# Loads on ACT's queue, stores on SyncE's queue, in a 180-degree rotation of images

## The chip, the cores and the metric

One core of one Trainium2 chip. The time is that of the core, in us of the device, measured over repeated executions; a profile is taken of one execution beside them and its span is about 2 us shorter than the time, since it begins with the first and ends with the last instruction. All runs quoted here are of the fast state, with a granted clock of 1.00, but for one execution, which is named where it comes.

## The reference

```python
batch, c, h, w = 32, 3, 256, 256          # float32
np.rot90(x, k=2, axes=(-2, -1))           # rotate every image by 180 degrees
```

Each of the 96 images of 65,536 elements is reversed as a flat list. 25.17 MB come in, 25.17 MB go out.

## The kernel before

A strip of 32 images lies in a tile of 128 partitions: each image is cut into 4 pieces of 16,384 elements (64 KiB), one per partition. Three strips (A, Bt, Ct) fill three tiles. VectorE reverses every partition in place, by swapping mirrored pieces of 2,048 elements through a small tile T. The store then puts the four pieces of an image in reversed order. Each tile is loaded once and stored once; no tile is used twice.

```python
    def load(t, g, lo, hi):
        return nc.sync.dma_start(out=t[:, lo:hi], in_=x4[g][:, lo:hi])

    def store(t, g):
        return nc.sync.dma_start(out=o4[g][:, ::-1, :], in_=t[:, :])

    def inside(t):                          # 12 copies on VectorE
        for lo in range(0, E // 2, J):
            hi = E - lo - J
            copy(T[:, :], back(t, hi, hi + J))
            copy(t[:, hi:hi + J], back(t, lo, lo + J))
            copy(t[:, lo:lo + J], T[:, :])

    TAIL = 1536
    load(A, 0, 0, E)
    load(Bt, 1, 0, E)
    body = load(Ct, 2, 0, E - TAIL)
    load(Ct, 2, E - TAIL, E)
    inside(A)
    first = store(A, 0)
    tc.add_manual_dep(                      # the hold: the first store waits for `body`
        first.ins, body.ins.name, ...)      # (arguments cut)
    for g, t in ((1, Bt), (2, Ct)):
        inside(t)
        store(t, g)
```

The load of Ct comes in two parts, a body of 58 KiB rows and a tail of 6 KiB rows. The first store is held until the body has landed, so that it gets going while the tail is on its way.

## Time and profile before

| | before |
|---|---|
| time, median of 6 runs | 122.25 us (122.0 to 122.47) |
| span of the profile | 120.2 us |
| DMA packets, share of 16 engines | 97.3%, one queue |
| VectorE busy | 37% |
| issue of the first store | 59.48 us |
| landing of the last store | 119.4 us |

In this trace a packet is one row of a transfer: the 1008 packets are 7 transfers of 128 rows and 112 packets of under 512 bytes. The prediction shows how the rows add up to the span. One more view is of use, the waits of SyncE's queue (columns: line, what it waited for, us in total, times, longest):

```profile
SPq L58 <- DMA Ct<-in_x_dram: 57.3, 2, 56.7
SPq L106 <- DMA out_dram<-Bt: 19.3, 1, 19.3
SPq L106 <- DMA out_dram<-Ct: 19.3, 1, 19.3
```

The first line is the hold: SyncE stands still for 56.7 us before it issues the first store. The other two are the end: the stores land one strip time, 19.3 us, apart.

### The profile page before, as it was taken

To read this page: it belongs to the slowest core of one execution; us is meant where nothing else is said; L and a number is where in the kernel's file an instruction comes from. 1 tells how busy PE (TensorE), PEld (TensorE's weight loads), DVE (VectorE), ACT (ScalarE), POOL (GpSimd) and SP (SyncE) were. 2 spreads that over 40 slices of the span, in tenths; PEclk is the share of its full clock that TensorE was granted. 3 is DMA by queue.
4 is the path that set the end of the run, shared out by engine and by line. 5 is a ranking of instruction groups with operands and counts; after the bars stand their busy time and mean duration, and the time that the engine had idled before them with its cause. 6 is when DMAs were issued, how large, how long until landed. Compare 5 with 4: busy or idle time off the path is not lost.

```text
span 120.2 us, 93 instructions
## 1 busy us (share of the span) xinstructions
DVE 44.2 (37%) x36; POOL 0.2 (0%) x4
## 2 busy tenths in 40 slices
DVE  0000000499995099999059999400000000000000
POOL 0000000000000000000000000000000000000000
DMA  9888988898889779779499888988898889888990
GB/s 349 349 349 371 676 349 349 371 676 349 349 349 698 316 316 632 316 336 613 202 408 698 349 349 349 698 349 349 349 698 349 349 349 698 349 349 349 632 414 0
DMA packets 1008, 50.33 MB, mean 419 GB/s; under 512 B 112, under 2 KB 112, under 8 KB 240
## 3 DMA queue, kind: packets, MB, share of 16 engines
q1 hardware_dynamic: 1008, 50.33, 97.3%
HBM read 25.17 MB, written 25.17 MB: 419 GB/s over the span
## 4 chain that ended last, share of the span: by engine, by line
DMA 34%; DVE 25%; another core or an unknown queue 4%; issue 1%; SPq 0%; DVEq 0%
DMA Bt<-in_x_dram 34%; DVE T L52 8%; DVE Bt L52 8%; DVE Ct L52 8%; SPq L55 0%; DVEq L52 0%
## 5 line engine op out<-in xcount | busy, mean ns | idle before, releaser
L52 DVE COPY T<-A 128x2048 f32<-128x2048 f32 x4 | 4.9, 1227 | 22.6 <-DMA A<-in_x_dram 22.5
L52 DVE COPY T<-Ct 128x2048 f32<-128x2048 f32 x4 | 4.9, 1227 | 4.5 <-DMA Ct<-in_x_dram 4.4
L52 DVE COPY T<-Bt 128x2048 f32<-128x2048 f32 x4 | 4.9, 1227 | 4.4 <-DMA Bt<-in_x_dram 4.3
L52 DVE COPY Bt<-T 128x2048 f32<-128x2048 f32 x4 | 4.9, 1227 | 0.1
L52 DVE COPY A<-T 128x2048 f32<-128x2048 f32 x4 | 4.9, 1227 | 0.1
L52 DVE COPY Ct<-T 128x2048 f32<-128x2048 f32 x4 | 4.9, 1227 | 0.1
L52 DVE COPY A<-A 128x2048 f32<-128x2048 f32 x4 | 4.9, 1227 | 0.1
L52 DVE COPY Bt<-Bt 128x2048 f32<-128x2048 f32 x4 | 4.9, 1227 | 0.1
L52 DVE COPY Ct<-Ct 128x2048 f32<-128x2048 f32 x4 | 4.9, 1226 | 0.1
L95 POOL MEMSET const-uint8-127<- 128x1 uint8 x1 | 0.1, 102 | 0.0
L95 POOL MEMSET const-bfloat16-1.0<- 128x1 bf16 x1 | 0.1, 101 | 0.0
L95 POOL MEMSET const-float32-0.0<- 128x1 f32 x1 | 0.1, 98 | 0.2 <-issue 0.2
L95 POOL MEMSET const-float32-1.0<- 128x1 f32 x1 | 0.1, 98 | 0.0
## 6 DMA issues: line engine op xcount, KB each, us to landing
Ct<-in_x_dram SPq DMA_DIRECT2D x1, 7424.0 KB, 57.7
Ct<-in_x_dram SPq DMA_DIRECT2D x1, 768.0 KB, 59.2
A<-in_x_dram SPq DMA_DIRECT2D x1, 21.8
Bt<-in_x_dram SPq DMA_DIRECT2D x1, 40.7
out_dram<-A SPq DMA_DIRECT2D x1, 21.3
out_dram<-Bt SPq DMA_DIRECT2D x1, 39.9
out_dram<-Ct SPq DMA_DIRECT2D x1, 42.9
```

The costliest lines, as they stand in the source:

```text
L52: tc.keep_in_program_order(nc.vector.tensor_copy(out=dst, in_=src))
L95: nc = _bacc.Bacc("TRN2", target_bir_lowering=False, num_devices=1)
```

## The change

Its intent: give loads and stores a queue each, so that neither stands behind the other. Order, sizes and the hold stay.

```diff
     def load(t, g, lo, hi):
-        return nc.sync.dma_start(out=t[:, lo:hi], in_=x4[g][:, lo:hi])
+        return nc.scalar.dma_start(out=t[:, lo:hi], in_=x4[g][:, lo:hi])
 
     def store(t, g):
-        return nc.sync.dma_start(out=o4[g][:, ::-1, :], in_=t[:, :])
+        return tc.keep_in_program_order(
+            nc.sync.dma_start(out=o4[g][:, ::-1, :], in_=t[:, :]))
```

The wrapper around the store keeps its place among the other instructions.

## The prediction

> **What bounds the kernel now.** I read the page from the top (busy time, the slices, the DMA queue), then the chain that ended last, then the issues with their landings, and last the windows around the two places that the change can touch: the first 2.6 us and the stretch from 58 to 61 us, where loading turns into storing.
>
> The head of the page and its DMA part:
>
> ```profile
> span 120.2 us, 93 instructions
> DVE 44.2 (37%) x36; POOL 0.2 (0%) x4
> q1 hardware_dynamic: 1008, 50.33, 97.3%
> HBM read 25.17 MB, written 25.17 MB: 419 GB/s over the span
> ```
>
> One queue carries all 50.33 MB, and its packets fill 97.3% of the time of the 16 DMA engines. VectorE, the only engine that computes, works 37%. So the bytes bound the kernel, not the copies. The part that lists the DMA issues, whose last number is us from issue to landing:
>
> ```profile
> Ct<-in_x_dram SPq DMA_DIRECT2D x1, 7424.0 KB, 57.7
> Ct<-in_x_dram SPq DMA_DIRECT2D x1, 768.0 KB, 59.2
> A<-in_x_dram SPq DMA_DIRECT2D x1, 21.8
> Bt<-in_x_dram SPq DMA_DIRECT2D x1, 40.7
> out_dram<-A SPq DMA_DIRECT2D x1, 21.3
> out_dram<-Bt SPq DMA_DIRECT2D x1, 39.9
> out_dram<-Ct SPq DMA_DIRECT2D x1, 42.9
> ```
>
> With the issue times of the timeline (loads at 0.73, 1.18 and, for both parts of Ct, from 1.64 on to about 2.1; stores at 59.48, 60.20, 76.51) the landings are: A 22.5, Bt 41.8, body of Ct 59.4, tail of Ct 61.3, then stores 80.8, 100.1, 119.4. Each strip takes 19.3 us, loading or storing. In the trace's DMA records one 65,536-byte row takes 2.42 us on its engine after the first few, and a strip gives each of the 16 engines 128 / 16 = 8 rows: 8 x 2.42 = 19.3. Six strips are 6 x 19.3 = 116 us. The other 4 us of the span are the start (first packet at about 1.7), slower first rows (up to 3.3 instead of 2.42 us) and the end (last landing 119.4, span end 120.2).
>
> The chain of waits shows the copies as a quarter of the span, and this must be read with care:
>
> ```profile
> DMA 34%; DVE 25%; another core or an unknown queue 4%; issue 1%; SPq 0%; DVEq 0%
> ```
>
> It follows Bt's load, then the copies in Bt and Ct, and breaks off at the last store. The copies of Ct end at 76.5, and store Ct is issued at once, but the engines are busy with store A until 80.8 and store Bt until 100.1. Store Ct needs its turn only at about 100. So Ct has some 100 - 76.5 - 1.1 (issue to first byte, below) = 22 us of slack, and the DVE share of this chain is not on the path that sets the end.
>
> The start, in the timeline and in windows (columns: stretch, length, DVE busy, POOL busy, clock, DMA share, GB/s; a packet is booked whole in the window in which it starts, so a share can exceed 1 and an empty window is not an idle engine):
>
> ```profile
> 0.73 0.39 SPq L55 DMA_DIRECT2D A<-in_x_dram  x1
> 1.40:1.60 0.20, 0.00 (x0) 0.00 (x0) 1.00 0.00 0
> 1.60:1.80 0.20, 0.00 (x0) 0.00 (x0) 1.00 2.95 983
> 1.80:2.00 0.20, 0.00 (x0) 0.00 (x0) 1.00 6.83 2294
> ```
>
> Issue at 0.73, first packets after 1.6: the DMA records put it at 1.03 us from issue to first packet, on an empty ring.
>
> The turn from loads to stores:
>
> ```profile
> 59.48 0.63 SPq L58 DMA_DIRECT2D out_dram<-A  x1
> 60.20:60.40 0.20, 0.00 (x0) 0.00 (x0) 1.00 0.88 369
> 60.40:60.60 0.20, 0.00 (x0) 0.00 (x0) 1.00 0.60 246
> 60.60:60.80 0.20, 0.00 (x0) 0.00 (x0) 1.00 4.04 1700
> 60.80:61.00 0.20, 0.00 (x0) 0.00 (x0) 1.00 8.52 3605
> ```
>
> The body of Ct landed at 59.4 and freed the first store, which was issued at 59.48. Through 60.2 to 60.6 the small rows (6,144 bytes, 0.234 us each) of the tail still start. From 60.6 on the 64 KiB rows of store A start. There is no empty window between: the 1.9 us tail (59.4 to 61.3) has hidden the latency of the first store. There is nothing left here to win by an earlier start: the store came into the ring just as the ring ran out of tail.
>
> **What the Trainium skill says.** (1) "DMA: Bandwidth & Descriptors", section "Issuing engines are not separate DMA queues": transfers that different engines issue run on the same 16 DMA engines and interleave, and issuing from two saves the sequencer's time to issue alone. The trace agrees as far as it can: an issue costs the queue 0.39 to 0.63 us and there are seven, all but the first off the path. (2) Same page, "Queues, rings and completion order": SyncE and ACT each own one ring on each DMA engine, and an engine goes round its rings packet by packet. The trace of before has one queue only, so no run here shows it yet; it matters for the tail, below. (3) "Perfetto Trace Analysis", section "DMA Optimizations", point 4, advises one issuing engine for inputs and another for outputs, above all in loops, to allow more dynamic spread. This kernel has no loop in which a load waits behind a store: all four loads are issued by 2.7 us, before the first store. So what that advice is for is absent. (4) "DMA: Bandwidth & Descriptors", "Latency and other measured facts", gives about 0.6 us from an issue of this kind to the first byte; this trace has 1.03, and I use that.
>
> **The change part by part.**
> - Loads on ACT. Removed from SyncE: four issues, from 0.73 to about 2.7 us; added to ACT: the same four. Only the first is on the path; ACT starts from the same barrier as SyncE and has nothing else to do, so its first issue should come within 0.1 us of 0.73. Rows, sizes and order are the same, so A, Bt and the body land within 0.1 to 0.2 us of where they did. Sum: 0 +- 0.15 us.
> - Stores on SyncE alone. SyncE now reaches its wait for the body at once instead of at 2.7 us, and then waits until 59.4 as before. Saved on the path: 0.
> - Hold of the first store. It waits for the landing of the body, now on another queue. That was already a semaphore wait (SyncE's queue waited 56.7 us for it), so its form and its cost stay: 0.
> - The turn. Store A's first packets are ready at 59.48 + 1.03 = 60.5, and by the windows the tail is nearly all started by 60.6. What is left then, none or one packet per engine, shares with rows of store A. If a row goes ahead of it, the tail's landing on that engine moves by one row, 2.4 us, from 61.3 to at most about 63.7; Ct's copies end at 78.9 instead of 76.5. Slack 22 us: 0 on the path. The bytes are the same and the engines never run out: 0.
> - Program order on the stores: the order of SyncE's instructions was already that; 0.
> - End: the last landing releases the same closing waits; 0.
>
> Sum: 0 +- 0.2 us, so 122.2, as the 122.18 before.
>
> **The rivals.** *The tail starves.* If the store's ring had work from the tail's beginning and engines alternated packet by packet, each of the 8 tail packets of an engine would wait for a 2.4 us row: up to 19 us later, at about 80.6. Then copies until 95.8 (15.2 us), first packet of store Ct ready at 96.9. That is still before 100: even this costs nothing, 122.2. It speaks against larger losses altogether.
>
> *Reads and writes overlap in an engine.* Two rings might let an engine read for one transfer while it writes for the other. Loads and stores meet only in the 1.9 us of the tail (of which the last 0.2 to 0.8 at most), so the gain is under 0.8 us, 1.9 if the whole tail were hidden: 121.4, or 120.3 at the very best, 1.5%. Against it: a row takes 2.42 us in either direction, which looks like one limit of the engine on bytes.
>
> *Switching rings costs a gap.* With one ring the store's rows stand behind the tail and start with no gap. If an engine needs time to take up another ring, or if the last tail packets and the first rows disturb each other as at the start (3.3 instead of 2.42 us for a row), up to 1 us is lost once: 123.2.
>
> *ACT starts late.* If ACT has work of its own ahead of its first issue, or its sequencer is slower with these, every landing moves by it. The profile shows no ACT instruction at all in 120 us, which speaks against it. A late start of 1 us would make 123.2; it would take 2.4 us to be over 2%.
>
> **Range and chances.** The three runs of before lie between 122.0 and 122.47, so the scatter is 0.25 us each way. The rivals that cost (gap, late start) reach 1 us and have perhaps one chance in six together; the overlap that gains 0.3 to 0.8 us perhaps one in eight. So 122.2, range 121.5 to 123.0. Over 2% means 2.4 us: no rival but a start that goes wrong gets there, and for a gain more would have to be won than the whole time in which both kinds of transfer are in flight. Faster 0.02, within 2% 0.95, slower 0.03.
>
> **What would show it right or wrong.** Two queues instead of one, with 25.17 MB each, and a summed share near 97%. The first load's issue at 0.7 to 0.9 us. Landings of A, Bt, body near 22.5, 41.8, 59.4; of the tail between 61.3 and 63.7; stores near 80.8, 100.1, 119.4. Copies of Ct end by 79 and store Ct is issued then. If the first load is issued over 0.3 us later, the step on ACT is wrong. If the tail lands after 64, the turn shares more than I say. If the distance from one store's landing to the next is not 19.3, the engines' rate has changed, and with it the ground of the whole prediction.

## The result, and the profile after

| | before | after |
|---|---|---|
| time, median of 6 runs | 122.25 us (122.0 to 122.47) | 122.18 us (122.08 to 122.54) |
| ratio of fast runs | | 0.9999, 95% interval 0.9982 to 1.0016 |

A ratio is the mean time of one kernel's fast runs over that of the other's of the same rounds, so it is not quite the ratio of the medians. The time did not change.

The head of the page after, and its queues (packets, MB, share of 16 engines):

```profile
span 120.3 us, 93 instructions
q10 hardware_dynamic: 576, 25.17, 49.0%
q1 hardware_dynamic: 432, 25.17, 48.4%
```

Two queues with half the bytes each, q10 with ACT's loads and q1 with SyncE's stores. Their shares make 97.4%, where one queue had 97.3%. The DMA issues after (last number: us to landing):

```profile
Ct<-in_x_dram ACTq DMA_DIRECT2D x1, 7424.0 KB, 57.8
Ct<-in_x_dram ACTq DMA_DIRECT2D x1, 768.0 KB, 59.2
A<-in_x_dram ACTq DMA_DIRECT2D x1, 21.8
Bt<-in_x_dram ACTq DMA_DIRECT2D x1, 40.7
out_dram<-A SPq DMA_DIRECT2D x1, 21.3
out_dram<-Bt SPq DMA_DIRECT2D x1, 39.9
out_dram<-Ct SPq DMA_DIRECT2D x1, 43.0
```

No landing is off by more than 0.1 us. The two issues that matter, in the timeline:

```profile
0.73 0.37 ACTq L55 DMA_DIRECT2D A<-in_x_dram  x1
59.50 0.64 SPq L59 DMA_DIRECT2D out_dram<-A  x1
```

ACT issues its first load at 0.73 us, as SyncE did. The turn from loads to stores, in the same windows as in the prediction:

```profile
60.20:60.40 0.20, 0.00 (x0) 0.00 (x0) 1.00 0.88 369
60.40:60.60 0.20, 0.00 (x0) 0.00 (x0) 1.00 0.73 307
60.60:60.80 0.20, 0.00 (x0) 0.00 (x0) 1.00 2.64 1106
60.80:61.00 0.20, 0.00 (x0) 0.00 (x0) 1.00 9.29 3932
```

The rows of store A start at the same moment as before. In the DMA records the last small row of the tail starts at 60.71 us and the first row of store A at 60.79 (before: 60.61 and 60.76). No row of the tail starts after one of the store, so on no engine did the two queues take turns. That it makes no difference for this reason that there are two queues is argued here; the experiments test it.

### The profile page after: what moved, and what is told of

It is laid out like the page before. It is cut to its first block, busy times and chain, and to the rows that moved or that the text cites. A ratio compares the mean times of both kernels' runs of the same rounds, so it can differ in the third digit from the quotient of the medians.

```text
span 120.3 us, 93 instructions
## 1 busy us (share of the span) xinstructions
DVE 44.2 (37%) x36; POOL 0.2 (0%) x4
## 4 chain that ended last, share of the span: by engine, by line
DMA 34%; DVE 25%; another core or an unknown queue 4%; issue 1%; ACTq 0%; DVEq 0%
DMA Bt<-in_x_dram 34%; DVE T L52 8%; DVE Ct L52 8%; DVE Bt L52 8%; ACTq L55 0%; DVEq L52 0%
```

## The experiments

The question is whether this reading is right: that two queues are harmless here because the hold keeps them from meeting, and that the bytes alone bound the kernel. All runs below were timed in 3 rounds beside the kernel before (122.05 to 122.17 us in these rounds); "two queues" means the kernel after. Where a rate is called spread, each row's bytes were spread evenly over its recorded duration. For the runs with a ratio below 1.02, where the 95% interval leaves out 1, the text calls it a small rise.

### Two queues without the hold

```diff
-    tc.add_manual_dep(first.ins, body.ins.name, ...)
```

> Two queues as in the change, the hold of the first store taken away (the store of A then goes when A's copies end, about 37.6 us). Theory (each engine alternates between its two rings packet by packet, whatever a packet's size): from about 38.7 us each load row waits for a 2.42 us row of a store; the body of Ct lands at about 84, each of the 8 small tail rows waits for a row too, so the tail lands only near 100, Ct's copies end near 116, store Ct ends near 136: about 139 us, slower by 14%. Rival 1 (the engines share by bytes): the tail lands at 81 to 85, the copies end by 100, time 122 to 124. Rival 2 (the rings do not compete, older work first): 122.2, and the hold has no use.

Measured: 148.78 us (147.53 to 149.64), ratio 1.217. The result is correct. Two of its DMA issues, with us to landing:

```profile
Ct<-in_x_dram ACTq DMA_DIRECT2D x1, 768.0 KB, 107.4
out_dram<-A SPq DMA_DIRECT2D x1, 50.7
```

The issue of the last store, in the timeline (start us, us):

```profile
124.80 0.54 SPq L59 DMA_DIRECT2D out_dram<-Ct  x1
```

Three windows (columns as in the prediction):

```profile
48.00:84.00 36.00, 8.95 (x8) 0.00 (x0) 1.00 1.00 375
84.00:104.00 20.00, 0.00 (x0) 0.00 (x0) 1.00 0.95 408
104.00:126.00 22.00, 14.72 (x12) 0.00 (x0) 1.00 0.07 28
```

The tail, 0.77 MB, landed at 2.1 + 107.4 = 109.5 us instead of 61.3. Each of its rows takes 0.234 us, but must wait for one 2.42 us row of a store. Between 86 and 103 us the DMA records hold 97 small rows and 102 store rows: one for one, although one has less than a tenth of the other's bytes. So the body landed at 88.3 us and the tail a further 21 us later, and the copies of Ct begin only then. While they run and store Ct gets under way, from 110 to 126 us, the engines are empty (last window).

Where the 26.5 us of span went, as engine time lost against 434 GB/s from the spread records, less what the kernel before loses: 16.0 us idle from 110 to 126, 4.3 us while the engines run dry one by one (103 to 110), 5.1 us of slower transfer from 48 to 84, 1.1 us as the stores set in (40 to 48). The mechanism was as expected; the size was not (139 expected). The expectation had neither the slow stretch nor the ragged end, and had the first store row at 38.7 us, where the records have 44.4.

### One queue without the hold

```diff
 # in the kernel before
-    tc.add_manual_dep(first.ins, body.ins.name, ...)
```

> The kernel before (one queue), the hold taken away. Theory: the store of A is issued at about 37.6 us but stands in the one ring behind all loads, so landings stay (tail 61.3, stores 80.8, 100.1, 119.4) and the time is 122.2. The rival that order between loads and stores is not kept in one ring: as in the two-queue run without hold, over 124.

Measured: 123.16 us (122.92 to 123.6), ratio 1.0093 (1.0070 to 1.0117). The issue of the tail, with us to landing:

```profile
Ct<-in_x_dram SPq DMA_DIRECT2D x1, 768.0 KB, 60.3
```

The tail lands at 62.4 us, where two queues had 109.5. Store A is issued at 37.69 us but its rows come after the tail, as one ring would have it; stores land at 81.7, 101.0, 120.4. So some 26 us of the run before come from having two queues and no hold together. But the time is 0.9% up, a small rise that was not expected. In the records the tail's small rows took up to 0.79 us instead of 0.234 with the stores queued directly behind them.

### Two queues, the hold kept, a longer tail

```diff
-    TAIL = 1536
+    TAIL = 8192
```

> Two queues, hold kept, but the last part of the load of Ct is 8192 elements a row instead of 1536, so that the first store is freed about 10 us before loading ends. This is my rival of the starving tail, made real. Packet by packet: from about 52 us each 1.21 us tail row waits for a 2.42 us store row, the tail lands at about 80.5, copies end at 95.8, the time stays 122.2. Shared by bytes: the tail lands at about 70. No sharing: at 61.3. In all three the time stays within 0.5 us of 122.2, because store Ct is not needed before 100.

Measured: 123.36 us (122.93 to 124.0), ratio 1.0102 (1.0065 to 1.0139). The profile's windows from the issue of store A (51.71 us) on:

```profile
52.00:58.00 6.00, 4.98 (x5) 0.00 (x0) 1.00 1.12 404
58.00:72.00 14.00, 0.00 (x0) 0.00 (x0) 1.00 1.05 456
```

The tail landed at 74.3, between the expectations of 80.5 (packet by packet) and 70 (by bytes), since the first store row did not start one us after its issue but between 56.4 and 59.0: four tail rows per engine had started by then. From then on the records show one for one again (59 to 70 us: 49 tail rows, 49 store rows). Store Ct was issued at 89.5, in time, and yet the time rose by 1%, more than the 0.5 us allowed. From 53 to 59 us the spread rate is 354 GB/s, which is 1.1 us lost; from 59 to 72 it is 434. So a tail that starves for 13 us costs nothing that shows by itself; the 1.1 us lost as the stores set in among the loads are about the whole rise.

### Loads and stores mixed all the way

Wrong result on purpose: all three stores write A as loaded.

```diff
-    inside(A)
-    first = store(A, 0)
-    ...                       # hold, copies and the other stores
+    for g in range(3):
+        store(A, g)
```

> Wrong result on purpose: all three stores write A as it was loaded, with no copy, from A's landing (22.5 us) on, beside the loads of Bt and Ct. Loads and stores then share the engines for tens of us. Theory (a DMA engine has one limit on bytes whichever way they go): the time stays at 122 (+- 1), and rows take longer from start to end or wait, with a total near 430 GB/s. Rival (reads for one ring overlap writes of the other): the total rate rises while both are in flight; at a full overlap the loads end at 61 and the stores at 81, about 83 us.

Measured: 123.74 us (123.29 to 124.07), ratio 1.0127 (1.0099 to 1.0154), 0.7 us above the range expected (122 +- 1). Windows of 32 and 30 us in which both queues have work:

```profile
28.00:60.00 32.00, 0.00 (x0) 1.00 0.99 430
66.00:96.00 30.00, 0.00 (x0) 1.00 0.99 430
```

(No DVE column, as VectorE has no instruction here.) The two directions together get 430 GB/s, as much as one alone. An engine that could read for one ring and write for another would have saved up to about 40 us (83 expected at a full overlap); nothing was saved. This disposes of the rival by which reads and writes overlap. Again about 1.0 us is lost as the stores set in (23 to 29 us, spread rate 362).

### What the small rows are worth

Two queues, no hold, Ct loaded in one piece (the removal of the hold is not shown again):

```diff
-    body = load(Ct, 2, 0, E - TAIL)
-    load(Ct, 2, E - TAIL, E)
+    load(Ct, 2, 0, E)
```

> Two queues, no hold, and Ct loaded in one piece (8 rows of 65,536 bytes on each engine, no small tail rows). Theory: most of the 22% that two queues without hold cost is the small tail rows, each of which waits for a 2.42 us store row; without them Ct lands when 8 rows of each kind are through, near 83 us at full rate, its copies end near 98, store Ct is in the ring before store Bt is done, no idle stretch, and the time is about 123.3 (with 1.1 us lost at the onset of the stores, as in the runs before); up to 130 if loads and stores go on at the 365 GB/s of the run with the small tail. Rival (mixing the two directions is itself what costs): the time stays near 148.

Measured: 131.99 us (131.55 to 132.74), ratio 1.081. The slow stretch, in the profile's windows:

```profile
48.00:84.00 36.00, 8.84 (x8) 0.00 (x0) 1.00 0.97 359
```

So without small rows most of the loss goes (148.8 to 132.0), though not to 123, nor to the 130 allowed for a slow mix: the spread rate from 48 to 84 us was 366 GB/s, much as in the run with the small tail (373), which costs 5.7 us, and Ct landed only at 90.6. Another 1.1 us went as the stores set in (40 to 48) and 1.2 us from 104 to 107, where some engines ran dry before store Ct's first rows.

The same in one queue (no hold, Ct in one piece):

> One queue, no hold, Ct loaded in one piece. Without the hold the one-queue kernel was 0.9% slower, and its small tail rows took about 0.5 us instead of 0.234 with the stores queued directly behind. Theory (the small rows suffer from the store behind them): with no small rows the time is 122.2 to 122.5. Rival (any turn from loads to stores queued in advance costs this much): 123.1.

Measured: 122.94 us (122.87 to 123.2), ratio 1.0064 (1.0044 to 1.0084). My theory, that the small rows suffer from the stores behind them, falls: without small rows the turn still costs. From 57 to 63 us the spread rate is 361 GB/s, 1.0 us lost, and rows at the turn took up to 3.6 us. So it is the turn itself, and it is no matter of two queues. (The 0.2 us less than with small rows may be theirs; the two intervals overlap.) In the kernels before and after, where the stores come as the loads run out, the turn loses only 0.2 to 0.3 us (60 to 64, spread), and of this 0.17 us before and 0.13 after is idle time of the engines (mean of the 16, 60.0 to 61.2), ahead of the first store rows.

### The hold moved behind the tail

```diff
-    load(Ct, 2, E - TAIL, E)
+    last = load(Ct, 2, E - TAIL, E)
...
-        first.ins, body.ins.name,
+        first.ins, last.ins.name,
```

> Two queues, the first store held until the tail has landed (61.3 us) instead of the body. Theory (the tail exactly hides the latency of the first store, and the engines stand empty without it): issue at 61.4, first packet 62.4 to 62.5, engines empty from 60.9 on, so 1.5 to 1.6 us lost: 123.7. Rival (the latency is hidden otherwise, the hold's place does not matter): 122.2.

Measured: 124.05 us (123.89 to 124.23), ratio 1.0146 (1.0124 to 1.0168). Windows around the turn:

```profile
60.40:61.20 0.80, 0.00 (x0) 0.00 (x0) 1.00 0.21 85
61.20:62.80 1.60, 1.07 (x1) 0.00 (x0) 1.00 0.00 0
62.80:63.20 0.40, 0.36 (x2) 0.00 (x0) 1.00 6.20 2621
```

This time the empty window is truly empty: the last tail row ends at about 61.2 and the first store rows start between 62.8 and 63.2. The time is 0.35 us over the 123.7 expected: the issue came at 61.70, and the first store row 1.28 us after it, where 1.03 was reckoned. So the tail does hide the latency of the first store, and the place of the hold is worth 1.8 us. It also means that the kernel before had already taken, but for the 0.2 to 0.3 us above, what a separate store queue could have given at the turn.

### Why some mixed stretches ran slower

Four runs bear on the 366 to 373 GB/s of the runs with two queues and no hold against the 434 of the mixed run. The first exchanges, in the run with two queues and no hold, the places in the output to which A and Bt go, so that the body of Ct runs beside another store region:

```diff
-    first = store(A, 0)
+    first = store(A, 1)
...
-        store(t, g)
+        store(t, {1: 0, 2: 2}[g])
```

> Wrong result on purpose: the run with two queues and no hold (148.8 us), with the places in the output of the stores of A and Bt exchanged. In that run body rows beside rows of store A moved only about 365 GB/s, in the mixed run with other pairs of places 434. Theory (which HBM places are read and written together decides): at 434 the body lands near 81, the tail near 102, the time is about 141. Rival (not the places, but that load and store rows are out of step between engines, or something else of that kernel): about 148.8 as before.

Measured: 149.23 us (148.78 to 150.45), ratio 1.223. Spread rate from 48 to 84 us 364: this exchange of places changes nothing.

The second leaves out the copies of Bt, from the run with two queues and no hold (`inside(t)` only for Ct):

> Wrong result on purpose: two queues, no hold (148.8 us), without VectorE's copies in Bt (42 to 57 us); those in A and Ct stay. That run moved about 365 GB/s while body rows of Ct and rows of store A alternated, the mixed run without any copies 434. Theory (VectorE's reading and writing of the on-chip memory slows or unsettles the mixed transfers): body beside store A at 434, body landing near 81, tail near 102, time about 141. Rival (the copies have nothing to do with it): about 148.8.

Measured: 148.61 us (147.16 to 149.72; the last of these, 1.7% above the fastest, counts as slow, at a clock of 1.00 like the rest; the median of the three fast ones is 147.89), ratio 1.213. Spread rate from 48 to 84 us 369, in a fast execution: not the copies of Bt.

The third adds 81 copies in T to the mixed run:

```diff
+    half = J // 2
+    copy(T[:, 0:half], A[:, half - 1::-1])
+    for k in range(40):
+        copy(T[:, half:J], T[:, half - 1::-1])
+        copy(T[:, 0:half], T[:, J - 1:half - 1:-1])
```

> Wrong result on purpose: the mixed run (123.7 us; loads beside stores of A, no copies) with 81 copies of 128x1024 on VectorE added in the small buffer T from A's landing on, some 50 us of them, on which no transfer waits. Theory as above: the stretch from 26 to about 75 us falls to about 365 GB/s and the time rises to 130 or more. Rival: 123.7.

Measured: 123.9 us (123.17 to 124.13), ratio 1.0134, beside 123.74 without the copies. One window:

```profile
28.00:60.00 32.00, 30.50 (x45) 0.00 (x0) 1.00 0.99 428
```

VectorE is busy 30.5 of 32 us and the transfers keep their rate. The theory that VectorE unsettles them is refuted from both sides, as far as these two runs go (the copies added here touch no tile that is in transfer, but for one read of A).

The fourth moves the hold to the landing of Bt, and with it the first store rows from 44.4 us to 46.3 and later, one or two rows (a correct result):

```diff
-        first.ins, body.ins.name,
+        first.ins, second.ins.name,     # second = load(Bt, 1, 0, E)
```

> Two queues, the first store held until Bt has landed (41.9 us) instead of going when A's copies end (37.8): the same mix of body rows and rows of store A as in the slow runs, which began with row 0 of both side by side, but started about two rows later in the load, as the fast mixed run did (its first store row came after two rows of a load). Theory 1 (each small tail row waits for a store row, packet by packet): between 8 tail rows lie 8 x 2.65 us, so the tail lands at 95 or later and the time is over 132. Theory 2 (which rows of load and store stand side by side decides the rate): 434 GB/s after an onset of 4 us, tail at about 95, time about 134. Rival to 2 (it is not that): about 365 GB/s again, tail near 102, time about 140.

Measured: 137.83 us (137.31 to 137.95), ratio 1.127. Two windows:

```profile
52.00:76.00 24.00, 4.93 (x5) 0.00 (x0) 1.00 0.97 420
76.00:96.00 20.00, 0.00 (x0) 0.00 (x0) 1.00 1.04 449
```

The spread rate from 52 to 95 us is 434 GB/s: the slow stretch is gone. The time was 4 us over the 134 expected, because the first store rows set in between 46.3 and 49.5 us, some engines thus one row later, and the tail landed at 98.8. In the four slow runs (no hold, two queues) the first store row came after one row of the load then in progress; in the four fast ones (this, the two mixed, the long tail) after two to four. So in eight runs the rate goes with the moment at which the stores set in, and this run, in which the hold alone was put back, at another place, shows that the moment matters. In the slow stretch the rows themselves take longer: in the run without the hold the 58 KiB rows that start from 48 to 84 us have a median of 2.78 us (up to 4.04), here, from 52 to 76, none takes over 2.19. Why, no run settles. That some engines load while others store is not enough: in the run with the longer tail both kinds were in progress at once, each on 3 or more of the 16 engines, for 80% of the time from 59 to 72 us, and the rate was 434. It could be which rows lie side by side.

### The queues exchanged

Loads on SyncE, stores on ACT, hold kept:

```diff
-        return nc.scalar.dma_start(out=t[:, lo:hi], in_=x4[g][:, lo:hi])
+        return nc.sync.dma_start(out=t[:, lo:hi], in_=x4[g][:, lo:hi])
...
-            nc.sync.dma_start(out=o4[g][:, ::-1, :], in_=t[:, :]))
+            nc.scalar.dma_start(out=o4[g][:, ::-1, :], in_=t[:, :]))
```

> The loads on SyncE and the stores on ACT, hold kept. Theory (the two issuing engines and their rings are alike, and nothing but the turn is shared): 122.2. Rival (ACT's ring or sequencer differs and happened to be hidden): over 0.5 us off.

Measured: 122.22 us (122.1 to 122.59), ratio 1.0016 (0.9993 to 1.0039). The two issuers are alike in this kernel.

No run beat the kernels before and after.

## Why the prediction was right

- *The first load on ACT comes no later.* Right: 0.73 us in both. The rival of a late start had nothing to it here; the exchanged queues agree.
- *The hold keeps its cost.* Right: the store is issued at 59.50 instead of 59.48.
- *At the turn, none or one packet of the tail is left beside the store.* Right, and it was none (60.71 against 60.79 us), partly by luck: the prediction had the first store row ready at 60.5, with the 1.03 us that it had read from the first load, and at 60.5 some engines still had a row of the tail to start. The store took 1.29 us from issue to first row, before and after. For the same reason it is not quite so that the engines never run out: they idle for 0.17 us before and 0.13 after, so that the difference stays near 0. The prediction called what is left at the turn a matter of slack, in that even a late tail would cost nothing. The runs show that it is more: without the hold the same two queues cost 22%.
- *A starving tail costs nothing, which speaks against larger losses altogether.* Half right. The longer tail did not let store Ct miss its turn, though the time rose by 1% from the stores' setting in. The sentence about larger losses was too wide: it holds for a store that starts with the tail. If the store is issued some 22 us earlier, the body is slowed too, the tail begins late, and the slack of 22 us is used up.
- *Reads and writes might overlap.* Refuted: 430 GB/s mixed, and no gain in the 62 us of the two windows.
- *Switching rings might cost up to 1 us.* In the change itself nothing of this was lost. Elsewhere a loss of this size came up, from another cause. Stores that come among or directly behind queued loads lose about 1 us, in two queues (1.1 us) as in one (1.0 us). With the hold as it stands 0.2 to 0.3 us are lost at the turn, before and after.
- *Engines bound by bytes.* Supported throughout: every mixed stretch stays, by spread rate, at or below the 434 GB/s of a single direction. The Trainium skill, "DMA: Bandwidth & Descriptors", section "Queues, rings and completion order", has engines go round their rings packet by packet; the runs now show it, row by row, with 97 small rows against 102 large ones.

## What to carry to other kernels

Splitting loads and stores over two queues gave nothing here, where the DMA engines are full and no load ever waits behind a store. It does take away the order that one queue gave for free: from then on, in these runs, an early store takes every second packet, and a late load of small rows, on which work depends, is drawn out to the pace of the store's large rows. If you split, hold the first store with an explicit wait, and place that wait so that its latency lies beside the last load.

## What the Trainium skill lacked or had wrong

- "DMA: Bandwidth & Descriptors", "Issuing engines are not separate DMA queues": it says that a second issuer saves the sequencer's issue time alone. In the change as it stands that agrees (ratio 0.9999). What it lacks is the harm: without the hold, two queues took 148.8 us and one queue 123.2.
- The same page, "Queues, rings and completion order": turns by packet agree with the runs, but the page's typical packet holds about 9 to 17 descriptors, and here the turn was a single row (49 tail rows against 49 store rows from 59 to 70 us in the run with the longer tail). It lacks what this means for rows of unequal size: 8 small rows per engine (0.234 us each, 1.9 us in all) took 21 us beside 2.42 us rows.
- The same page, "Latency and other measured facts": about 0.6 us to the first byte. Here 1.0 us on an empty ring from the issue of the first load to its first row (1.04 before, 1.01 after), 1.29 us for the held first store in both, and 4.4 to 6.6 us from the issue of a store to the start of its first row in the runs where loads of 32 to 64 KiB rows were in flight on the other ring.
- "Perfetto Trace Analysis", "DMA Optimizations", point 4 (one engine for inputs, another for outputs): it lacks a word that the order between the two is then lost.
- "SBUF — State Buffer", "Who interferes with whom": that DMA does not contend with a compute engine agrees: 428 GB/s beside 30.5 us of copies in 32, 430 without.
- No page has that stores which set in among or right behind queued loads lose about 1 us once (0.9 to 1.2 us by spread rate in eight runs with two queues and one with one), or that mixed loads and stores run at 434 GB/s or at 364 to 373, depending on when the stores set in.
